# A hybrid decoder layer: the recurrence's output norm a block sooner, the matrix memory's norm turned into rows and spread by one-pass products

## The chip, the core and the metric

The kernel runs on one core of one Trainium2 chip. The metric is the time of one execution on the device in microseconds (us), median of several runs. A core has five engines that run beside each other, each through its own list of instructions in order: TensorE (PE, matrix products; PEld are its weight loads), VectorE (DVE), ScalarE (ACT), GpSimd (POOL) and SyncE (SP, which here only issues DMA transfers). They wait for each other by semaphores. Products land in PSUM, all else lives in SBUF.

## What is computed

One inference step of a decoder layer for 256 prompt tokens and 8 sample tokens, 264 columns together, model width 2048, all in float32. The reference, cut to the part that the change touches:

```python
z = rmsnorm(x, g_mix) @ w_in                       # one projection for all groups
h_rg, h_last = rglru(...)                          # gated linear recurrence, width 1024
y_rg = rmsnorm(h_rg * gelu(z[..., OFF_RGG:OFF_Q]), g_rg_out)
h_ml, C_new, n_new, m_new = mlstm(q, k, v, logi, logf, C0, n0, m0)   # 4 heads of 256
h_ml = rmsnorm(h_ml, g_ml_out.reshape(ML_HEADS, ML_DV))              # per token and head
y_ml = h_ml * jax.nn.sigmoid(z[..., OFF_O:OFF_I])
x = x + jnp.concatenate([y_rg, y_ml], axis=-1) @ w_out
```

Behind it come cross-attention to 256 memory tokens, a SwiGLU and a final norm. Two norms matter here: the one over the recurrence's 1024 channels, a number per token, and the one over the matrix memory's 256 channels, a number per token and head.

## The kernel before

Activations lie transposed, channels on the 128 partitions and the 264 tokens along the row. The weights stream through in steps: a list `steps` holds one entry for each block of 128 output channels, and the loop over it (L1430) loads a block two or three steps ahead, splits the block of the next step into a high and a low part that PE takes in one pass (`split_half`, L193: ACT makes the high part, DVE subtracts to get the low one, in two halves of 8 chunks each), runs the step's products, and then pumps side work. A block is 16 chunks of three products, `mm3`: high by high, high by low, low by high. So a step is 48 products of 128 by 264.

Steps 25 to 32 are the recurrence's gate blocks, 33 to 40 the matrix memory's output gates (`evac_o`, j = 0 to 7), and step 41 begins `w_out`, whose right side is the normed recurrence (chunks 0 to 7, `yrg`) and the gated matrix memory (chunks 8 to 15, `yml`).

Work that belongs to no block runs as generators beside the loop (`side`, `pump`). A yielded `STEP` ends a generator's turn; a number lets it go on if the engines' priced clocks have room. Products that such work needs are put between the chunks of a block through `later(f, after=n)` and `drip` (L282, L287): a function waits until n more chunks were recorded, is then recorded right there, and the next product of the block is ordered behind it. What is recorded is put into each engine's order by a list scheduler with its own estimates, except on SP, where it stays as written. The engines then keep that order.

The generators that matter:

- `rg_out` (L588): the recurrence's norm. `rstd_wide` (L384) splits the sum of squares `acc_rg` into halves, sums over the partitions by two products with a matrix of ones (the products stand in the program wherever the generator is pumped), and takes the inverse root by 9 DVE steps on 128x264. Then each of the 8 blocks is scaled and split into `yrg`.
- `ml_norm` (L873): the matrix memory's norm. Squares are summed per head in `a`; `sums(h)` brings the sums over the partitions, tokens on partitions, into 12 columns; the last `sums` forms f, a 128x12 vector (4 heads by 3 token windows), by a chain of short DVE operations. Behind it `spread` (L359) brings f back along the rows for each head: products of a broadcast column with the identity, 128x128, 128x128 and 128x8, in float32, each issued as two instructions. The 8 blocks of `hT` are scaled from PSUM.
- the loop keeps finished products in `pend` and runs their evacuation at the start of the next step, except where i is in a short list (L1440).

PSUM has four banks for blocks (`mm`) and four for side work (`ax`). Weight halves have four buffers (`W`), their raw loads five.

Of the kernel before, what the change touches and what calls it, by code (L numbers as in the profile page):

```python
# [10 lines left out]
F32 = mybir.dt.float32  # L11
F32R = mybir.dt.float32r
I32 = mybir.dt.int32
AF = mybir.ActivationFunctionType
# [3 lines left out]
P = 128  # L18
D = 2048
KC = D // P  # L20
T = 256
NS = 8
N = T + NS
RGB = 8
H = 4
# [19 lines left out]
STEP = object()  # L45
# [45 lines left out]
def layer_kernel(ctx: ExitStack, tc, xT, memT, vec, wrg, w_in, w_out, w_q, w_k, w_v, w_o,  # L91
# [3 lines left out]
    act, dve, pe = Engine(nc.scalar, price_act), Engine(nc.vector, price_dve), Engine(nc.tensor, price_pe)  # L95
# [10 lines left out]
    def nm(s):  # L106
        uid[0] += 1
        return f"{s}_{uid[0]}"
# [9 lines left out]
    def B(shape, dt=F32, skip=0):  # L118
        return view(sb.tile([P, SLOT], dt, tag="B", bufs=NB, name=nm("B")), shape, skip)
# [51 lines left out]
    steps = []  # L171
    LD, LS = 3, 1
    GATES = 8

    raws, splits = {}, {}

# [58 lines left out]
    st = {}  # L235
# [46 lines left out]
    def later(*fs, after=0):  # L282
        k = [after, list(fs)]
        drips.append(k)
        return k
# [13 lines left out]
    def bank(tag="mm"):  # L299
        return psm.tile([P, 512], F32, tag=tag, bufs=4, name=nm(tag))  # L300
# [4 lines left out]
    ident = const.tile([P, P], F32, name="ident")  # L305
# [3 lines left out]
    ones_r = const.tile([P, P], F32R, name="ones_r")  # L309
    dve.tensor_copy(ones_r, ones)  # L310
    ident_r = const.tile([4, H], F32R, name="ident_r")
# [47 lines left out]
    def spread(ps, c, n=N):  # L359

        for j in range(2 if n == T else 3):
            lo, hi = (j * P, j * P + P) if j < 2 else (T, N)
            i = pe.matmul(ps[:, lo:hi], c[j].to_broadcast([P, P]), ident[:, P - (hi - lo):], start=True, stop=True)
        return i
# [19 lines left out]
    def rstd_wide(acc, y, n):  # L384

        w = acc.shape[-1]
        hl, vt = B([P, 2, w], F32R), B([P, 3, w])
        act.activation(hl[:, 0], acc, AF.Copy)
        dve.tensor_sub(hl[:, 1], acc, hl[:, 0].bitcast(F32))
        yield STEP  # L390
        ps = bank("ax")
        for k in range(2):
            pe.matmul(ps[:, :w], ones_r, hl[:, k], start=k == 0, stop=k == 1)
        v, i, t = vt[:, 0], vt[:, 1].bitcast(I32), vt[:, 2]
        dve.tensor_scalar(v, ps[:, :w], 1.0 / n, EPS, op0=OP.mult, op1=OP.add)
        dve.tensor_single_scalar(i, v.bitcast(I32), 1, op=OP.logical_shift_right)
        dve.tensor_scalar(y.bitcast(I32), i, -1.0, 1597463007.0, op0=OP.mult, op1=OP.add)
        for _ in range(3):
            dve.tensor_mul(t, y, y)
            dve.scalar_tensor_tensor(t, t, -0.5, v, op0=OP.mult, op1=OP.mult)  # L400
            dve.scalar_tensor_tensor(y, t, 1.5, y, op0=OP.add, op1=OP.mult)
        yield 0.1

    def sumsq(acc, x, first):
        if first:
# [168 lines left out]
    acc_rg = const.tile([P, N], F32, name="acc_rg")  # L574
# [11 lines left out]
        return f  # L586

    def rg_out():  # L588
        yield STEP
        rr = ltmp()  # L590
        yield from rstd_wide(acc_rg, rr, RGB * P)
        st["yrg"] = HL(RGB)
        for n in range(RGB):
            h = rg["h"](n)
            dve.tensor_mul(h, h, rr)
            split(*st["yrg"](n), h, V("g_rg", n))
            yield 0.75


    ml = {}  # L600
# [272 lines left out]
    def ml_norm():  # L873

        while not (ml["pg"].done and ml["sg"].done) or st["i"] < 33:
            yield STEP
        hh = hT["t"]
        a = B([P, H, N])
        for h in range(H):
            for vb in range(2):  # L880
                act.activation(hh(2 * h + vb)[:, T:N], nums[:, 2 * h + vb, :], AF.Copy)
            sumsq(a[:, h, :], hh(2 * h), True)
            sumsq(a[:, h, :], hh(2 * h + 1), False)
            yield 0.35
        yield STEP
        ps = bank("ax")
        r, v, f = ctile(12), ctile(12), ctile(12)

        def sums(h):
            i = token_sums(ps, a[:, h, :], 3 * h)  # L890
            if h == 0:
                dve.tensor_max(r.rearrange("p (h j) -> p j h", j=3), den.rearrange("p (h j) -> p j h", j=3),
                               emc.rearrange("p (j h) -> p j h", h=H))
                dve.reciprocal(r, r)
                dve.tensor_mul(v, r, r)
            if h == H - 1:
                dve.scalar_tensor_tensor(v, ps[:, 0:12], 1.0 / 256, v, op0=OP.mult, op1=OP.mult)
                dve.tensor_scalar(v, v, EPS, None, op0=OP.add)
                rsqrt(v, f)
                dve.tensor_mul(f, f, r)  # L900
            return i

        for h in range(H):
            k = later(lambda h=h: sums(h), after=3 if h else 1)
        while k[1]:
            yield STEP
        for h in range(H):
            ps = bank("ax")
            spread(ps, [f[:, 3 * h + j: 3 * h + j + 1] for j in range(3)])
            for vb in range(2):  # L910
                dve.tensor_mul(hh(2 * h + vb), hh(2 * h + vb), ps[:, :N])
            yield 0.7
            ml["nn"] = h + 1

    def evac_o(j):
        def f(ps):
# [512 lines left out]
    pend = []  # L1429
    for i, (src, cols, pef, evf, need) in enumerate(steps):  # L1430
        load_piece(i + LD - 1)
        if i == 5:
            st["rg"] = side(rg_gen(), 0)
        if i == 6:
            finish(lambda: fn.done)
        for q in need:
            if q in st:
                finish(lambda: st[q].done)
        st["i"] = i
        if i not in (4, 5, 34, 35):  # L1440
            with tc.high_priority(300):
                for e, x in pend:
                    e(x)
            pend = []
        now = pe.clock
        dve.clock, act.clock = max(dve.clock, now), max(act.clock, now)
        parts = 2 if i == 0 else 1
        split_half(i + LS, 0, parts)
        if i + LS < len(steps) and steps[i + LS][1] > 1024:
            split_half(i + LS, 1, parts)  # L1450
        ps = pef(i)
        if 1 <= i < 4:
            with tc.issue_after(st["split"].ins):
                for q in ((0, 1), (2,), (3,))[i - 1]:
                    square(q)
        if i == 3:
            fn = side(first_norm(), -1)
        if i == 6:
            with tc.issue_after(st["split"].ins), tc.issue_after(st["low"].ins):
                rg_coef()  # L1460
        if evf is not None:
            pend.append((evf, ps))
        load_piece(i + LD)
        pump(pe.clock + SLACK)
        if i == 24:
            ml["ng"] = side(ml_norm(), -1)
        if i == len(steps) - 12:
            state_load()
        if i == 40:
            st["memg"] = side(mem_gen(), 7)  # L1470
# [4 lines left out]
    for lo, hi in ((0, 1), (1, 2), (2, 4), (4, 6), (6, 8), (8, 10), (10, 12), (12, 16)):  # L1475
        if lo == 12:
            state_store(3, 4)
        for c in range(lo, hi):
            e, r = (pool_e, rstd) if c in POOLC else (dve, fin["ps"][:, :N])
# [108 lines left out]
```

## Time and profile before

| | |
|---|---|
| three runs | 1541.16, 1540.39, 1539.16 us; median 1540.39 |
| the profiled execution's own time | 1540.57 us |
| its span (first to last instruction) | 1538.7 us |
| granted TensorE clock, mean | 0.997 |
| DMA | 329.17 MB, 214 GB/s on average |

In a row of a timeline stand start and duration in us, the engine, the program's line, the operation, what it writes and reads (tile names without numbers), the count, and in brackets the idle time before it with what ended it. In the chain of waits, the work that ended last is followed back from the end; its rows are start, duration, engine, tile and count. L63 is the line of a helper that records all instructions, so tile names and shapes tell them apart: `mm` is a block's PSUM bank, `ax` one of side work, `W` a split weight half, `raw` its load, `c` a tile of up to 16 columns, `t` and `lt` row tiles, `B` the large buffers. Durations of neighbouring rows of one engine overlap a little: the next starts before the former is written out.

### The profile page before, as it was taken

Reading aid. Unit: us, or ns where it says so; the run is one execution under the profiler, and the core shown is the slowest. Engines: PE = TensorE matmul, PEld = TensorE weight load, DVE = VectorE, ACT = ScalarE, POOL = GpSimd, SP = SyncE. Lnnn points to the kernel's source line nnn. Section 1 sums busy time; section 2 is a strip of 40 time slices with the busy share of each in tenths; the row PEclk is TensorE's granted clock in tenths of the full one; section 3 lists DMA queues with packets and bytes.
Section 4 is the critical chain, followed back from the end, with each engine's and each line's share of the span. In section 5 each row is a group of like instructions: output and inputs, shape, how many; then the busy total and the mean of one; then the engine's idle time right before and its main releaser. Section 6 shows DMA issues by size and latency. Waiting matters only on the chain.

```text
span 1538.7 us, 30018 instructions
## 1 busy us (share of the span) xinstructions
PE 1525.9 (99%) x12040; PEld 1492.1 (97%) x12040; DVE 1059.1 (69%) x2012; ACT 783.0 (51%) x1233; POOL 129.9 (8%) x195
## 2 busy tenths in 40 slices
PE   8999999999999999999999999999999999999997
PEld 8999999999998888899999999999999999999997
DVE  7976798878898989966665555455555554555554
ACT  6455775655555666654444443334444433344463
POOL 0001220000234334400000000000000000000000
PEclk9999999999999999999999999999999999999999
DMA  8655897556789798745555555555555555555473
GB/s 293 197 165 186 291 326 246 182 183 231 261 331 333 244 346 325 256 159 193 183 181 186 183 184 186 180 190 180 183 187 179 186 184 181 189 179 184 159 225 119
DMA packets 93659, 329.17 MB, mean 214 GB/s; under 512 B 10992, under 2 KB 11936, under 8 KB 93520
## 3 DMA queue, kind: packets, MB, share of 16 engines
q1 hardware_dynamic: 77760, 272.51, 53.0%
q0 software_dynamic: 15472, 54.22, 9.8%
q8 instruction: 94, 1.54, 0.4%
q10 hardware_dynamic: 288, 0.53, 0.1%
q14 instruction: 45, 0.37, 0.1%
HBM read 314.36 MB, written 12.86 MB: 213 GB/s over the span
## 4 chain that ended last, share of the span: by engine, by line
PE 97%; DVE 1%; DMA 1%; issue 0%; ACT 0%; POOL 0%; ACTq 0%; DVEq 0%
PE mm L63 92%; PE ax L63 5%; DVE B L63 1%; DMA B<-scr 0%; DMA xres<-xT 0%; DVE W L63 0%; DVE t L63 0%; ACT B L63 0%; POOL B L846 0%; ACTq L304 0%; DVE lt L63 0%; DVEq L1565 0%; ACT W L63 0%; ACT L63 0%; DVEq L63 0%
## 5 line engine op out<-in xcount | busy, mean ns | idle before, releaser
L63 PE MATMUL mm<-B,W 128*128 128x264 f32 (+2 forms) x11008 | 1363.3, 285 | 0.4 <-DVE W L63 0.4
L63 PEld LDWEIGHTS mm<-B,W 128*128 128x128 f32 x11008 | 1340.6, 188 | 12.3 <-DVE W L63 0.6
L63 ACT ACTIVATE W<-raw 128x1024 fp32r<-128x1024 f32 (+2 forms) x520 | 536.5, 1034 | 641.2 <-PE mm L63 438.5
L63 DVE TENSOR_TENSOR W<-raw,W 128x1024 fp32r<-128x1024 f32 (+2 forms) x520 | 620.4, 1195 | 348.8 <-ACT W L63 347.6
L63 PE MATMUL mm<-W,B 128*128 128x512 f32 x384 | 92.4, 395 | 0.0
L63 PEld LDWEIGHTS mm<-W,B 128*128 128x128 f32 x384 | 70.9, 188 | 16.2
L63 DVE TENSOR_TENSOR t<-mm,rstd 128x264 f32<-128x264 f32 x104 | 44.9, 433 | 43.8 <-PE mm L63 43.6
L1480 POOL TENSOR_TENSOR B<-B,rstd 128x264 f32<-128x264 f32 x4 | 2.8, 738 | 854.1 <-ACT rstd L63 854.1
L63 DVE TENSOR_TENSOR xres<-xres,mm 128x264 f32<-128x264 f32 (+1 forms) x81 | 34.3, 425 | 34.8 <-PE mm L63 34.7
L63 DVE SCALAR_TENSOR_TENSOR B<-B,dw 128x256 f32<-128x256 f32 x128 | 53.9, 477 | 1.8 <-ACT dw L63 1.7
L63 DVE SCALAR_TENSOR_TENSOR dw<-B,qsm,dw 128x256 f32<-128x256 f32 x96 | 50.7, 538 | 0.4
L1115 POOL TENSOR_TENSOR dr<-dw,dr 128x256 fp32r<-128x256 f32 x32 | 38.7, 1209 | 103.2 <-ACT dr L63 103.1
L63 PE MATMUL ax<-B,B 128*128 128x256 f32 (+2 forms) x272 | 44.7, 303 | 0.0
L63 PEld LDWEIGHTS ax<-B,B 128*128 128x128 f32 x272 | 38.5, 190 | 2.4
L63 ACT ACTIVATE B<-xres,vecs 128x264 fp32r<-128x264 f32 (+1 forms) x64 | 31.0, 502 | 2.2 <-DMA xres<-xT 2.0
L1104 POOL DMA_DIRECT2D B<-kcT x32 | 17.4, 543 | 134.8 <-DVE B L63 126.5
L63 ACT ACTIVATE t<-t 128x264 f32<-128x264 f32 (+1 forms) x61 | 24.7, 407 | 4.5 <-DVE t L63 4.5
L63 ACT ACTIVATE B<-t 128x264 fp32r<-128x264 f32 (+1 forms) x60 | 24.5, 408 | 4.5 <-DVE t L63 4.5
L63 ACT ACTIVATE t<-B,B 128x128 f32<-128x128 f32 x64 | 20.2, 388 | 12.0 <-DMA B<-scr 12.0
L63 ACT ACTIVATE t<-xres 128x264 f32<-128x264 f32 (+2 forms) x46 | 18.8, 410 | 14.6 <-DVE xres L63 14.6
L63 ACT ACTIVATE dw<-B,qsm 128x256 f32<-128x256 f32 x32 | 16.2, 508 | 18.3 <-DVE B L63 8.9
L63 DVE SCALAR_TENSOR_TENSOR B<-xres,vecs,B 128x264 fp32r<-128x264 f32 x48 | 22.4, 490 | 1.9 <-ACT B L63 1.9
(168 smaller groups left out, 663.6 us busy)
## 6 DMA issues: line engine op xcount, KB each, us to landing
raw<-w_gu SPq DMA_DIRECT2D x176, 512.0 KB, 3.6
raw<-w_d SPq DMA_DIRECT2D x80, 512.0 KB, 3.7
raw<-w_in SPq DMA_DIRECT2D x78, 512.0 KB, 5.0
raw<-w_out SPq DMA_DIRECT2D x32, 512.0 KB, 3.7
raw<-w_q SPq DMA_DIRECT2D x32, 512.0 KB, 5.4
B<-kcT POOLq DMA_DIRECT2D x32, 512.0 KB, 7.9
B<-vcT POOLq DMA_DIRECT2D x32, 512.0 KB, 8.3
raw<-w_k SPq DMA_DIRECT2D x32, 512.0 KB, 6.3
```

The source lines that it names most:

```text
L63: return f(*a, **k)
L1104: pool_e.dma_start(kc, kcT[h, b])
L1115: pool_e.tensor_sub(wr[:, 1], acc, wr[:, 0].bitcast(F32))
L1480: e.tensor_mul(st["y"](c), st["y"](c), r)
```

## The change

Five edits. In `rstd_wide` the generator yields its last product, so that it can be recorded as a drip. `rg_out` makes the halves at once, then records products and inverse root 13 chunks later by a drip; its eight scalings wait for the steps in `RGAT` and are ordered behind the latest weight split. `ml_norm` puts all four sums two chunks apart; 19 further chunks on, `turn` brings f from columns to rows, a 4x264 tile, by three products with the identity, ACT and DVE split it into halves, and from six chunks later `scale(h)` spreads each head by two one-pass products of 4 rows, and scales its two blocks. The loop holds the evacuation of steps 33, 34 and 35 until the products of step 36 are recorded.

```diff
@@ -171,6 +171,7 @@
     steps = []
     LD, LS = 3, 1
     GATES = 8
+    RGAT = (34, 34, 34, 37, 38, 38, 39, 39)
 
     raws, splits = {}, {}
 
@@ -390,7 +391,7 @@
         yield STEP
         ps = bank("ax")
         for k in range(2):
-            pe.matmul(ps[:, :w], ones_r, hl[:, k], start=k == 0, stop=k == 1)
+            last = pe.matmul(ps[:, :w], ones_r, hl[:, k], start=k == 0, stop=k == 1)
         v, i, t = vt[:, 0], vt[:, 1].bitcast(I32), vt[:, 2]
         dve.tensor_scalar(v, ps[:, :w], 1.0 / n, EPS, op0=OP.mult, op1=OP.add)
         dve.tensor_single_scalar(i, v.bitcast(I32), 1, op=OP.logical_shift_right)
@@ -399,7 +400,7 @@
             dve.tensor_mul(t, y, y)
             dve.scalar_tensor_tensor(t, t, -0.5, v, op0=OP.mult, op1=OP.mult)
             dve.scalar_tensor_tensor(y, t, 1.5, y, op0=OP.add, op1=OP.mult)
-        yield 0.1
+        yield last
 
     def sumsq(acc, x, first):
         if first:
@@ -586,13 +587,19 @@
         return f
 
     def rg_out():
-        yield STEP
         rr = ltmp()
-        yield from rstd_wide(acc_rg, rr, RGB * P)
+        wide = rstd_wide(acc_rg, rr, RGB * P)
+        next(wide)
+        k = later(lambda: next(wide), after=13)
+        while k[1]:
+            yield STEP
         st["yrg"] = HL(RGB)
         for n in range(RGB):
+            while st["i"] < RGAT[n]:
+                yield STEP
             h = rg["h"](n)
-            dve.tensor_mul(h, h, rr)
+            with tc.issue_after(st["low"].ins):
+                dve.tensor_mul(h, h, rr)
             split(*st["yrg"](n), h, V("g_rg", n))
             yield 0.75
 
@@ -900,17 +907,37 @@
                 dve.tensor_mul(f, f, r)
             return i
 
+        fp = bank("ax")
+        hl = B([P, 2, N], F32R)[0:4]
+
+        def turn():
+            fj = f.rearrange("p (h j) -> p j h", j=3)
+            for j, w0 in enumerate((0, P, T)):
+                w = min(P, N - w0)
+                i = pe.matmul(fp[0:4, w0: w0 + w], fj[:, j, :], ident[:, P - w:], start=True, stop=True)
+            act.activation(hl[:, 0], fp[0:4, :N], AF.Copy)
+            dve.tensor_sub(hl[:, 1], fp[0:4, :N], hl[:, 0].bitcast(F32))
+            return i
+
+        def scale(h):
+            ps = bank("ax")
+            sel = ident_r[:, h: h + 1].to_broadcast([4, P])
+            for k in range(2):
+                i = pe.matmul(ps[:, :N], sel, hl[:, k], start=k == 0, stop=k == 1)
+            with tc.issue_after(st["low"].ins):
+                for vb in range(2):
+                    dve.tensor_mul(hh(2 * h + vb), hh(2 * h + vb), ps[:, :N])
+            ml["nn"] = h + 1
+            return i
+
         for h in range(H):
-            k = later(lambda h=h: sums(h), after=3 if h else 1)
+            later(lambda h=h: sums(h), after=1)
+        for h in range(H):
+            if h == 0:
+                later(turn, after=19)
+            k = later(lambda h=h: scale(h), after=1 if h else 6)
         while k[1]:
             yield STEP
-        for h in range(H):
-            ps = bank("ax")
-            spread(ps, [f[:, 3 * h + j: 3 * h + j + 1] for j in range(3)])
-            for vb in range(2):
-                dve.tensor_mul(hh(2 * h + vb), hh(2 * h + vb), ps[:, :N])
-            yield 0.7
-            ml["nn"] = h + 1
 
     def evac_o(j):
         def f(ps):
@@ -1437,7 +1464,7 @@
             if q in st:
                 finish(lambda: st[q].done)
         st["i"] = i
-        if i not in (4, 5, 34, 35):
+        if i not in (4, 5, 34, 35, 36):
             with tc.high_priority(300):
                 for e, x in pend:
                     e(x)
@@ -1449,6 +1476,11 @@
         if i + LS < len(steps) and steps[i + LS][1] > 1024:
             split_half(i + LS, 1, parts)
         ps = pef(i)
+        if i == 36:
+            with tc.high_priority(300):
+                for e, x in pend:
+                    e(x)
+            pend = []
         if 1 <= i < 4:
             with tc.issue_after(st["split"].ins):
                 for q in ((0, 1), (2,), (3,))[i - 1]:
```

What the scheduler makes of it, engine by engine. Numbers behind names tell buffers apart. In PE's list `mm_359` is the block of step 34, `ax` a side bank, `ones_r` the matrix of ones. Before, PE has the recurrence's two products in step 37 (block `mm_393`), behind its first half:

```order
L63 MATMUL mm_393_3327<-B_17_165,W_383_3245 128x264
L63 MATMUL mm_393_3327<-B_16_164,W_383_3245 128x264
L63 MATMUL ax_377_3210<-B_364_3092,ones_r_78 128x264 [waits DVE_49,PE_49]
L63 MATMUL ax_377_3210<-B_364_3092,ones_r_78 128x264
L63 MATMUL mm_393_3327<-B_18_174,W_384_3248 128x264 [waits Activation_49]
```

Now they stand in step 34, six products before its end:

```order
L63 MATMUL mm_359_3039<-B_21_185,W_345_2947 128x264
L63 MATMUL mm_359_3039<-B_20_184,W_345_2947 128x264
L63 MATMUL ax_360_3082<-B_355_3029,ones_r_78 128x264 [waits PE_49,Activation_49]
L63 MATMUL ax_360_3082<-B_355_3029,ones_r_78 128x264 [waits DVE_49]
L63 MATMUL mm_359_3039<-B_20_184,W_345_2947 128x264
L63 MATMUL mm_359_3039<-B_21_185,W_345_2947 128x264
```

The pair moved three steps up; the second product has a wait of its own for DVE.

DVE's list, the end of the chain that makes f (`c_362`, now `c_366`). Before, one weight split (`W_384`) stands in the chain's second half:

```order
L63 SCALAR_TENSOR_TENSOR c_362_3090<-c_370_3165,c_362_3090 128x12 [waits DVE_49]
L63 TENSOR_TENSOR c_370_3165<-c_362_3090 128x12 [waits DVE_49]
L63 TENSOR_TENSOR W_384_3248<-raw_358_3085,W_384_3248 128x8x128 [waits DMAHW0_49,Activation_49]
L63 SCALAR_TENSOR_TENSOR c_370_3165<-c_370_3165,c_361_3089 128x12 [waits DVE_49]
L63 SCALAR_TENSOR_TENSOR c_362_3090<-c_370_3165,c_362_3090 128x12 [waits DVE_49]
```

Now the recurrence's inverse root and three of its scalings (`B_184`, `B_370`) and two splits (`W_379`, `W_393`) stand in it, and the 4x264 subtraction follows:

```order
L63 SCALAR_TENSOR_TENSOR B_370_3115<-B_184_1700,vecs_68,B_369_3114 128x264 [waits Activation_49]
L63 SCALAR_TENSOR_TENSOR c_375_3169<-c_375_3169,c_365_3109 128x12 [waits DVE_49]
L63 TENSOR_TENSOR W_379_3217<-raw_362_3105,W_379_3217 128x8x128 [waits DMAHW0_49,Activation_49]
L63 SCALAR_TENSOR_TENSOR c_366_3110<-c_375_3169,c_366_3110 128x12 [waits DVE_49]
L63 SCALAR_TENSOR_TENSOR B_370_3115<-B_184_1700,vecs_68,B_369_3114 128x264 [waits Activation_49] x2
L63 TENSOR_TENSOR c_375_3169<-c_366_3110 128x12 [waits DVE_49]
L63 SCALAR_TENSOR_TENSOR c_375_3169<-c_375_3169,c_365_3109 128x12 [waits DVE_49]
L63 TENSOR_TENSOR W_393_3324<-raw_376_3204,W_393_3324 128x8x128 [waits DMAHW1_49,Activation_49]
L63 SCALAR_TENSOR_TENSOR c_366_3110<-c_375_3169,c_366_3110 128x12 [waits DVE_49]
```

So the recurrence's work moved from behind f to ahead of it and between its steps; the order of DVE, ACT and PE up to the pair in step 34 is the same in both kernels.

PE's list at the start of `w_out`. Before, products of step 42 (`mm_432`) stand among those of step 41 (`mm_421`):

```order
L63 MATMUL mm_421_3606<-B_389_3306,W_413_3535 128x264 [waits DVE_49]
L63 MATMUL mm_421_3606<-B_388_3305,W_413_3535 128x264
L63 MATMUL mm_421_3606<-B_396_3384,W_413_3535 128x264 [waits Activation_49]
L63 MATMUL mm_432_3679<-B_388_3305,W_419_3600 128x264 [waits DVE_49]
L63 MATMUL mm_432_3679<-B_388_3305,W_419_3600 128x264
L63 MATMUL mm_432_3679<-B_389_3306,W_419_3600 128x264
```

Now step 41 (`mm_423`) runs on at that place:

```order
L63 MATMUL mm_423_3609<-B_370_3115,W_415_3538 128x264
L63 MATMUL mm_423_3609<-B_369_3114,W_415_3538 128x264
L63 MATMUL mm_423_3609<-B_406_3454,W_415_3538 128x264
L63 MATMUL mm_423_3609<-B_407_3455,W_415_3538 128x264
L63 MATMUL mm_423_3609<-B_406_3454,W_415_3538 128x264 x2
```

The mixing of the two blocks moved to the last two gate chunks of step 41; past it PE's list is the old one again. SP's and POOL's lists are the same.

## The prediction

> **What bounds the kernel now.** I read the page first, then who PE waits for, then the chain of waits and the engines' timelines around the edited steps.
>
> ```profile
> span 1538.7 us, 30018 instructions
> PE 1525.9 (99%) x12040; PEld 1492.1 (97%) x12040; DVE 1059.1 (69%) x2012; ACT 783.0 (51%) x1233; POOL 129.9 (8%) x195
> PE mm L63 <- DVE W L63: 0.4, 1, 0.4
> ```
>
> TensorE (PE) is busy 99% of the span. Away from start and end it idles at two places, 0.6 us near 163 us and 0.4 us near 279 us. So the change can win only what it takes off PE's own stream plus that 0.4 us, and every new PE wait adds in full. The chain around the edited steps is all PE:
>
> ```profile
> 201.62 35.49 PE mm L63 x294
> 237.11 0.56 PE ax L63 x6
> 237.67 1.56 PE mm L63 x12
> ...
> 243.49 0.56 PE ax L63 x6
> 244.05 7.20 PE mm L63 x59
> 251.25 2.58 PE ax L63 x24
> 253.82 2.38 PE mm L63 x19
> 256.20 0.24 PE ax L63 x2
> 256.44 14.38 PE mm L63 x120
> ```
>
> A block product takes 35.49/294 = 0.1207 us, a block of 48 takes 5.79. The first x6 group is the first of four norm sums and stands 6 products into step 35, so step 35 starts at 236.39 and step 34 at 230.60. Behind the last sum 6 products remain, so step 36 starts at 244.77 and step 37 at 250.56. Step 37 holds the x24 group (matrix-memory spread, 2.58) and the x2 group (recurrence norm, 0.24); step 38 starts at 256.44 + 24 x 0.1207 = 259.34.
>
> **The recurrence norm, moved from step 37 into step 34.** Its two products now stand behind 42 of step 34's 48: PE is there at 237.11 - 12 x 0.1207 = 235.66. They read the high and low half of the recurrence's sum of squares.
>
> ```profile
> 234.89 0.41 ACT L63 ACTIVATE B<-acc_rg 128x264 fp32r<-128x264 f32 x1
> 235.69 1.22 DVE L63 TENSOR_TENSOR W<-raw,W 128x1024 fp32r<-128x1024 f32 x1
> 236.82 0.43 DVE L63 TENSOR_TENSOR B<-acc_rg,B 128x264 fp32r<-128x264 f32 x1
> 238.01 1.23 DVE L63 TENSOR_TENSOR W<-raw,W 128x1024 fp32r<-128x1024 f32 x1 [0.75 <-ACT W L63]
> 278.79 21.44 PE L63 MATMUL mm<-B,W 128*128 128x264 f32 x176 [0.42 <-DVE W L63]
> ```
>
> The high half is there at 235.30. The low half is not: VectorE (DVE) makes it behind a weight split, until 237.25, and up to this row DVE, ACT and PE have the same order in both kernels. Before, the product came 19 us later and this was hidden. Now the second product waits for it. PE gets there at 235.78 and goes on at 237.30 (0.05 after the operation, as behind the split of 277.51 that ends at 278.74): **stall 1 is 1.5 us**, between 1.4 and 1.7. All of PE's stream is queued behind it.
>
> **The matrix-memory norm.** The four sums now stand two chunks apart, the same four interruptions. The vector f behind them is a chain of 14 short DVE operations; before it was ready at 248.4, 2.8 us ahead of its use:
>
> ```profile
> 244.29 0.59 DVE L63 TENSOR_SCALAR c<-c 128x12 f32<-128x12 f32 x3
> 248.23 0.17 DVE L63 TENSOR_TENSOR c<-c,c 128x12 f32<-128x12 f32 x1
> 258.53 0.49 DVE L63 SCALAR_TENSOR_TENSOR B<-t,vecs,B 128x264 fp32r<-128x264 f32 x1
> 258.94 0.30 DVE L63 TENSOR_SCALAR B<-B 128x264 int32<-128x264 int32 x1
> 259.14 1.30 DVE L63 SCALAR_TENSOR_TENSOR B<-t,vecs,B 128x264 fp32r<-128x264 f32 x3
> 260.36 0.43 DVE L63 TENSOR_TENSOR t<-mm,rstd 128x264 f32<-128x264 f32 x1
> 260.70 0.29 DVE L63 TENSOR_SCALAR lt<-B 128x264 int32<-128x264 int32 x1
> 260.90 1.23 DVE L63 TENSOR_TENSOR W<-raw,W 128x1024 fp32r<-128x1024 f32 x1
> 262.04 0.43 DVE L63 TENSOR_TENSOR B<-lt 128x264 f32<-128x264 f32 x1
> 265.45 0.42 DVE L63 TENSOR_TENSOR B<-lt 128x264 f32<-128x264 f32 x1
> 265.91 0.43 DVE L63 SCALAR_TENSOR_TENSOR B<-B 128x264 f32<-128x264 f32 x1
> ```
>
> In the new order DVE runs, from 238.01 to f: 5 weight splits at 1.14 (260.90 to 262.04), 5.70; 7 wide steps whose successor needs them at 0.46 (265.45 to 265.91), 3.22; 8 other wide ones at 0.345 (260.36 to 260.70), 2.76; 3 with a gain vector at 0.41 (258.53 to 258.94), 1.23; 2 integer ones, 0.5; 5 short ones at 0.2 (0.59 for three dependent), 1.0, and nine between other work, 0.8 in all (0.09 is the part of the 0.17 that isn't overlapped). The sum is 15.2, **f ready at 253.25**. DVE never pauses there: by the same count its splits' ACT halves, the sums and step 35's end come 0.1 to 1.5 us before they are needed.
>
> PE reaches the turn, 36 products into step 36, at 237.42 + 6 x 0.1207 + (244.77 - 236.39) + 36 x 0.1207 = 250.87. It waits to 253.3, and as f is the weights here a load of 0.19 follows, which can't run ahead (its row stands below): **stall 2 is 2.6 us**. If short operations cost nothing and nothing waits in the chain, it is 1.2; if every short one takes 0.2 and each wait adds some, 3.4. I take the count.
>
> **PE's own work.** Out goes the x24 group: steps 37 and 38 are 8.78 apart, 48 products 5.79, the x2 group 0.24, so it and its interruption cost 2.75. In come a turn of 6 instructions and 8 one-pass products; the latter's nearest rows, 4 rows of weights on 256 columns:
>
> ```profile
> 147.10 0.29 PEld L63 LDWEIGHTS ax<-B,ident_r 4*128 4x128 f32 x2
> 147.10 0.50 PE L63 MATMUL ax<-B,ident_r 4*128 4x256 f32 x2
> 147.53 0.92 PE L63 MATMUL ax<-B,B 128*128 128x256 f32 x4
> L63 PEld LDWEIGHTS ax<-ident,c 128*128 128x128 f32 x48 | 5.7, 190 | 0.3 <-DVE c L63 0.3
> ```
>
> A pair holds PE 0.43 instead of 0.24, but its two loads follow each other within 0.11, so the extra is paid on entering and leaving. Eight in a row: 8 x 0.12 + 0.28 = 1.25; between 0.96 and 1.75 (8 x 0.215). The turn: 6 at 2.58/24 = 0.1075 and 0.15 for the interruption, 0.8; between 0.2 and 0.95. Net -0.7, between -1.6 and 0.
>
> The Trainium skill, "TensorE: Matmul & The Clock Gate", section "LDWEIGHTS (loading the stationary operand)", says a weight load takes time by its columns and not by its rows. The spread's 0.1075 per instruction agrees with its 107 ns for 128 columns; the turn's weights have 4 columns, and by the rule it would cost about 0.3 (an estimate by that page) in place of 0.8, the sum 0.5 less.
>
> **The wait at 279.** Before, a product of step 42 stood inside step 41 and waited for its weights' low half behind the recurrence's scalings. In the new order step 41 runs through first and the scalings lie over steps 36 to 39: -0.4. What is late next: each later split is due at least 2 us before PE by the same count (step 39's first done at 264, used at 268).
>
> **At nothing.** One more small copy and subtraction (0.41 and 0.43, as the rows of 234.89 and 236.82) lie under the 12 products between turn and scaling, with 0.3 us to spare; without that cover 0.8. The eight scalings only move. Gates held till step 36: their block's bank is needed again three steps later. POOL's last two memory-token loads wait for later buffers, but are read only after step 43. The moved parts issue no transfer; SP's weight loads wait for splits that come a few us later and have over 10 us left.
>
> **Sum.** 1.5 + 2.6 - 0.7 - 0.4 = +3.0, against the profiled execution's own 1540.57 us (span 1538.7) 1543.6, against the median of 1540.39 1543.4; I say **1543.5**. About 0.2% (3.08 us) is what a measurement of this kernel can tell from no change, and the forecast lies on that line. By the ends of the terms it is +0.7 to +5.1.
>
> **Rivals.**
> Not slower: f is in time. If DVE's queue to f is 2 us or more shorter than counted, stall 2 shrinks to its weight load or a little more and the sum is +0.2 to +1, 1541.2. It decides where DVE reaches f by 250.9. For it: before, f took 4.3 us with one split in its way. Against: five splits and the whole recurrence norm now lie ahead, and DVE's queue is in order.
>
> Clearly slower: the clock. At the start of the span PE ran slow:
>
> ```profile
> 6.40:12.00 5.60, 3.93 (x18) 3.73 (x19) 4.62 (x11) 4.95 (x12) 0.00 (x0) 0.70 1.01 361
> 8.46 3.99 PE ax L63 x19
> ```
>
> The granted clock was 0.70 there and a product took 0.21. If stall 2 brings that back for as many products, 19 x 0.09 = 1.7 more, 1545.2; it decides from a stall of a length that no row here shows (0.6 us at 163 did nothing). The page named above, "Part 1: The HAM clock gate", has the clock fall after an idle window of about 3.4 us; by that rule 2.6 us isn't enough, which is why this stays a small rival.
>
> The change does what it says: no stall at either place, only -0.7 - 0.4, 1539.3. Against it stands the low half's row at 236.82.
>
> **How the numbers follow.** Forecast 0.70 (1541.9 to 1545, half of it beyond the line), f in time 0.13, clock 0.13, neither stall 0.04. Slower by over 0.2%: 0.36 + 0.13 = 0.49; faster 0.03, only if a gain I don't see joins the last case; the rest 0.48 is within. The range 1541.1 to 1545.7 takes in the terms' ends but for the corners, the upper rival and most of the lower.
>
> **What would show it.** In PE's waits, after: one of 1.5 us for DVE on B near 236 and one of 2 to 3 for DVE on c near 251; none near 279; x24 gone, an x6 and an x8 group around 254 to 257. Wrong if PE's waits stay under 1 us, if step 38 starts before 261, or if the granted clock dips.

## The result and the profile after

| | before | changed |
|---|---|---|
| median in the same series | 1540.74 us (8 runs, 1539.16 to 1541.28) | 1544.47 us (8 runs, 1541.12 to 1547.05) |
| ratio, 95% interval | | 1.0025 (1.0015 to 1.0034), that is +3.9 us (+2.3 to +5.2) |
| the profiled execution | 1540.57 us, span 1538.7 | 1543.46 us, span 1541.7 |

All medians and ratios here are of runs in the faster of the two states in which this program runs; of all experiments only the pair later had others, two of its eleven runs (1663.11 and 2529.84 us).

The page of the changed kernel, its span and engines:

```profile
span 1541.7 us, 29995 instructions
PE 1526.2 (99%) x12030; PEld 1491.8 (97%) x12030; DVE 1059.3 (69%) x2013; ACT 784.1 (51%) x1234; POOL 129.3 (8%) x195
```

PE is busy almost as long as before (1526.2 against 1525.9 us); most of the 3.0 us of span is idle time. PE's waits in the changed kernel (total in us, times, longest):

```profile
PE ax L63 <- ACT B L63: 2.9, 1, 2.9
PE ax L63 <- DVE c L63: 2.2, 1, 2.2
PE ax L63 <- DVE B L63: 1.2, 2, 0.7
```

The wait for DVE on `W` near 279 is gone, the one for `c`, which holds f, is new. PE's timeline at the two edited places:

```profile
236.69 0.29 PE L63 MATMUL ax<-B,ones_r 128*128 128x264 f32 x1
237.47 0.39 PE L63 MATMUL ax<-B,ones_r 128*128 128x264 f32 x1 [0.49 <-DVE B L63]
...
253.56 0.63 PE L63 MATMUL ax<-ident,c 128*4 128x128 f32 x6 [2.20 <-DVE c L63]
254.12 1.70 PE L63 MATMUL mm<-B,W 128*128 128x264 f32 x12
255.76 1.22 PE L63 MATMUL ax<-B,ident_r 4*128 4x264 f32 x8
256.91 43.29 PE L63 MATMUL mm<-B,W 128*128 128x264 f32 x359
```

And DVE's, the low half, the split behind it, and the last operation of f:

```profile
236.98 0.43 DVE L63 TENSOR_TENSOR B<-acc_rg,B 128x264 fp32r<-128x264 f32 x1
238.17 1.23 DVE L63 TENSOR_TENSOR W<-raw,W 128x1024 fp32r<-128x1024 f32 x1 [0.76 <-ACT W L63]
253.24 0.17 DVE L63 TENSOR_TENSOR c<-c,c 128x12 f32<-128x12 f32 x1
```

Both stalls are where the prediction put them: 0.49 us at the pair, 2.20 at the turn. f came at 253.41 (forecast 253.25). The turn, the spreading and what they interrupt take 256.91 - 253.56 less 12 products of 0.1207, 1.9 us, where the x24 group took 2.75: 0.8 less.

Yet these don't add up to a plain 3.0. PE reached the pair 1.2 us later than the same place stood in before, although all engines have one order up to there. So the executions differ ahead of the change, and the spans alone don't tell what it costs. A second profile of each kernel, and those of the experiments, tell more. I take the start of step 34 from each profile, and the time from there to the end of the span:

| kernel | span | step 34 starts | from there to the end | against before | low half, after that start |
|---|---|---|---|---|---|
| before | 1538.7 | 230.60 | 1308.1 | | 6.65 |
| before, again | 1540.2 | 232.12 | 1308.1 | 0.0 | 5.26 |
| changed | 1541.7 | 231.79 | 1309.9 | +1.8 | 5.62 |
| changed, again | 1542.6 | 233.58 | 1309.0 | +0.9 | 3.05 |
| changed, third | 1541.0 | 231.07 | 1309.9 | +1.8 | 5.60 |
| changed, fourth | 1541.5 | 230.94 | 1310.6 | +2.5 | 4.58 |
| scalings later | 1538.4 | 231.46 | 1306.9 | -1.2 | 4.60 |
| both later, the turn too | 1537.9 | 230.96 | 1306.9 | -1.2 | 4.86 |
| pair and scalings later | 1537.1 | 228.84 | 1308.3 | +0.2 | 5.14 |
| recurrence only | 1539.2 | 231.11 | 1308.1 | 0.0 | 5.65 |
| twelve products | 1540.7 | 231.85 | 1308.9 | +0.8 | 3.91 |
| pair later | 1542.7 | 230.86 | 1311.8 | +3.7 | 5.26 |
| turn early | 1543.7 | 230.62 | 1313.1 | +5.0 | 3.98 |
| turn early, PE busy | 1541.9 | 230.29 | 1311.6 | +3.5 | 4.36 |

The start is that of the recurrence's pair in PE's timeline, plus 0.17 (the chain of waits of the kernel with twelve products has at 236.92 what the timeline has at 236.75), less the products of 0.1207 ahead of it: 42, or 51 or 54 where an experiment moved the pair. For before it is the prediction's 230.60, and for its second profile 1.52 more, as its first x6 group shows below. The last column is the end of DVE's row `B<-acc_rg,B`, less that start.

### The profile page after: what moved, and what is told of

It reads as the page before. It is cut to its first block, busy times and chain, and to the rows that moved or that the text cites. A ratio compares the mean times of both kernels' runs of the same rounds, so it can differ in the third digit from the quotient of the medians.

```text
span 1541.7 us, 29995 instructions
## 1 busy us (share of the span) xinstructions
PE 1526.2 (99%) x12030; PEld 1491.8 (97%) x12030; DVE 1059.3 (69%) x2013; ACT 784.1 (51%) x1234; POOL 129.3 (8%) x195
## 4 chain that ended last, share of the span: by engine, by line
PE 94%; DVE 2%; DMA 2%; issue 1%; ACT 1%; ACTq 0%; POOL 0%; DVEq 0%
PE mm L63 90%; PE ax L63 5%; DMA B<-scr 1%; DVE B L63 1%; DVE W L63 1%; DVE t L63 0%; DMA xres<-xT 0%; ACT W L63 0%; ACT t L63 0%; ACT B L63 0%; DVE c L63 0%; DVE lt L63 0%; DVE acc_rg L63 0%; POOL B L853 0%; ACTq L305 0%
```

## The experiments

**The scalings later.** The first three scalings of the recurrence out of f's way, the products where they were.

```diff
-    RGAT = (34, 34, 34, 37, 38, 38, 39, 39)
+    RGAT = (37, 37, 37, 37, 38, 38, 39, 39)
```

> The changed kernel, with its first three scalings of the recurrence held until step 37 (RGAT begins 37, 37, 37 in place of 34, 34, 34). On DVE three scalings with 128x264 products, three with the gain vector and one weight split then stand behind f and no longer ahead of it; the products keep their order. By the count of the prediction f is ready at 250.0 in place of 253.3, and PE is at the turn at 250.9 or later. Theory: PE starts the turn when DVE has f, so the wait for DVE on c falls from 2.2 us to under 0.3; the wait for the low half near 237 stays as it was (0.5 to 1.5, by how late PE gets there). Time 1541.2 (1540.7 to 1542.0), that is 2.2 to 3.2 less than the changed kernel. Rival, that the 3.4 us lost at the turn come from something else (the products of four weight columns, the banks, the gates held): the time stays at 1543 or above and the wait for c, or an idle stretch at that place, stays over 1.5 us.

Measured: 1539.35 us, ratio 0.9992 (0.9983 to 1.0001). PE's timeline, and DVE's for the end of f:

```profile
236.36 0.41 PE L63 MATMUL ax<-B,ones_r 128*128 128x264 f32 x2
250.19 0.64 PE L63 MATMUL ax<-ident,c 128*4 128x128 f32 x6
```

```profile
248.97 0.17 DVE L63 TENSOR_TENSOR c<-c,c 128x12 f32<-128x12 f32 x1
```

f is there at 249.1, a microsecond ahead of PE, and both waits are gone. What is left of the change is -1.2 from step 34 on: the prediction's -0.4 and the measured -0.8. So the turn, the four columns, the banks and the held gates cost nothing that shows; the wait for f does. Against the expectation, which had 1540.7 to 1542.0, the first wait went too, since in this execution the low half came 1 us earlier against PE than in the changed kernel's first profile. With the scalings one weight split, the last ahead of f, moved behind f as well; what it does shows further down.

**The recurrence's half alone.** The new `rg_out` and `RGAT`, with `ml_norm` and the hold of the gates as before.

```diff
-        if i not in (4, 5, 34, 35, 36):
+        if i not in (4, 5, 34, 35):
...
+            spread(ps, [f[:, 3 * h + j: 3 * h + j + 1] for j in range(3)])
```

> The recurrence's half of the change alone: its two products in step 34, its root and its scalings at the steps of RGAT. The matrix memory's norm is that of before (float32 spread, now at the end of step 37), and so is the hold of the gates. DVE's list to f is as long as in the changed kernel, but PE needs f only at the end of step 37, at about 258, with f ready at 255.4 by the count. Theory, the wait for c comes from needing f 36 products into step 36, not from the recurrence's work as such: no wait for c over 0.3 us, a wait for B near 237 of 0 to 1.5 us (more where PE arrives early against DVE), none near 279. From the start of step 34 to the end that is -0.4 to +1.1 us against before, time 1540.3 to 1541.8, ratio 0.9997 to 1.0007. Rival, that the recurrence's move costs what the changed kernel loses, wherever f is needed: 1543 or more.

Measured: 1539.52 us, ratio 0.9992 (0.9982 to 1.0002). PE's timeline, then DVE's:

```profile
236.01 0.29 PE L63 MATMUL ax<-B,ones_r 128*128 128x264 f32 x1
236.82 0.39 PE L63 MATMUL ax<-B,ones_r 128*128 128x264 f32 x1 [0.53 <-DVE B L63]
...
257.75 2.74 PE L63 MATMUL ax<-ident,c 128*128 128x128 f32 x24
```

```profile
255.03 0.17 DVE L63 TENSOR_TENSOR c<-c,c 128x12 f32<-128x12 f32 x1
```

f comes even later, at 255.2, and PE doesn't wait for it: it needs it at 257.75. From step 34 on the kernel is even with before: 0.53 lost at the pair, 0.4 won at 279. The time is 0.8 us below the range that I expected; from step 34 on it is within it. The recurrence's move by itself is nearly free. It costs where the matrix memory's f stands behind it in DVE's queue and is needed in step 36.

**The pair later.** Do the two stalls add up?

```diff
-        k = later(lambda: next(wide), after=13)
+        k = later(lambda: next(wide), after=16)
-                later(turn, after=19)
+                later(turn, after=16)
```

> The changed kernel, with the recurrence's two products three chunks later (after=13 becomes 16), the sums and the turn shifted with them so that the turn stands 30 products into step 36 in place of 36. PE then gets to the pair when the low half is ready or nearly so. Rival, the two stalls add up, as the prediction's sum has them: the first stall goes, the second stays at about 2.2 to 2.6 us, and the time falls by 0.5 to 1.5 us against the changed kernel. Theory, both stalls end at a time that DVE's list sets, so that an earlier stall only shortens the later one: the wait for B near 237 falls under 0.4, the wait for c grows to 3 to 4.5 us, and the time is that of the changed kernel or up to 1.0 us more (six more products lie behind f, 0.7 us): 1543.8 to 1545.5. If the wait for c is over 3.4 us the granted clock may also show a dip behind it.

Measured: 1544.46 us (median of nine runs), ratio 1.0027 (1.0017 to 1.0038), within what the theory expected and the same as the changed kernel's 1544.47. PE's timeline, a window of 6 us around it (length, busy time and instructions of PE, PEld, DVE, ACT, POOL, then the granted clock and the DMAs), and DVE's end of f:

```profile
236.85 0.40 PE L63 MATMUL ax<-B,ones_r 128*128 128x264 f32 x2
252.39 1.05 PE L63 MATMUL ax<-ident,c 128*4 128x128 f32 x6 [3.46 <-DVE c L63]
253.37 3.44 PE L63 MATMUL mm<-B,W 128*128 128x264 f32 x18
```

```profile
249.00:255.00 6.00, 2.61 (x13) 2.26 (x14) 3.46 (x12) 0.75 (x2) 0.00 (x0) 0.77 0.53 175
```

```profile
252.08 0.17 DVE L63 TENSOR_TENSOR c<-c,c 128x12 f32<-128x12 f32 x1
```

The wait at the pair is gone and nothing is won: f came 15.4 us after DVE began the split behind the low half (236.87 to 252.25), as in the changed kernel's first profile (238.17 to 253.41, 15.2). PE, with 15 products fewer between pair and turn, waits that much longer. So in these two executions f is timed by DVE's queue, and moving the turn forward only moves the wait. The second finding wasn't in the sum: behind 3.46 us of idle time the granted clock was 0.77, the turn took 1.05 us in place of 0.63, and 18 products took 3.4 us in place of 2.2.

**Twelve products ahead of the turn.** PE works in the time in which it would wait.

```diff
         def turn():
             fj = f.rearrange("p (h j) -> p j h", j=3)
+            for _ in range(12):
+                pe.matmul(fp[:, :N], ones_r, st["xn"](0)[0], start=True, stop=True)
```

> The changed kernel, with twelve extra products of 128x264 by the matrix of ones recorded directly ahead of the turn; they are written to the bank that the turn overwrites. PE's own work grows by 12 x 0.1207 = 1.45 us, and all engines but PE have the order of the changed kernel. Theory, f sets the time: the wait for c falls from 2.2 to about 0.75 us and the time stays within 0.3 us of the changed kernel. Rival, PE's own work counts and the wait is moved along: the wait for c stays at 2.2 us and the time is 1.45 us more. A third: if the long idle stretch of PE costs clock afterwards, the shorter wait makes this kernel faster than the changed one, by up to 1.5 us.

Measured: 1542.48 us, ratio 1.0011 (1.0002 to 1.0020). PE's timeline, and a row of its chain of waits for the pair:

```profile
236.75 0.41 PE L63 MATMUL ax<-B,ones_r 128*128 128x264 f32 x2
250.49 1.61 PE L63 MATMUL ax<-B,ones_r 128*128 128x264 f32 x12
252.58 0.64 PE L63 MATMUL ax<-ident,c 128*4 128x128 f32 x6 [0.47 <-DVE c L63]
```

```profile
236.92 0.24 PE ax L63 x2
```

The wait shrank to 0.47, and from step 34 on the kernel is no slower than the changed one (+0.8 against +0.9 to +2.5): 1.45 us of added work are hidden. Its median lies 2.0 and 0.9 us below those of the changed kernel in two other series, on the side of the third expectation, but the intervals of the ratios overlap (1.0002 to 1.0020 here, 1.0015 to 1.0034 and 1.0007 to 1.0025 there).

**The pair and the scalings later.** Both waits were to go.

```diff
-    RGAT = (34, 34, 34, 37, 38, 38, 39, 39)
+    RGAT = (37, 37, 37, 37, 38, 38, 39, 39)
-        k = later(lambda: next(wide), after=13)
+        k = later(lambda: next(wide), after=17)
-                later(turn, after=19)
+                later(turn, after=17)
```

> The changed kernel, with the first three scalings held until step 37 and the recurrence's two products four chunks later (after=17), the turn kept at 36 products into step 36. By the count of the prediction the low half is there 0.2 us ahead of the pair and f is ready at about 250.4, ahead of PE at 250.9. Theory: neither wait is left (each under 0.3 us), PE's own work is 0.8 us less than before and the wait near 279 stays gone: 1539.5 (1538.8 to 1540.4), 0.4 to 1.6 us less than before the change and some 4 to 5 less than the changed kernel. Rival: a wait for a weight split or for a scaled block turns up behind step 37, since eleven wide operations now stand there in DVE's list, and the time is 1540.5 to 1542.

Measured: 1540.12 us, ratio 0.9996 (0.9987 to 1.0005). The time is within what I expected, but the wait for c, which was to be under 0.3 us, was 1.20. PE's timeline, then DVE's:

```profile
248.87 0.63 PE L63 MATMUL ax<-ident,c 128*4 128x128 f32 x6 [1.20 <-DVE c L63]
```

```profile
247.41 1.23 DVE L63 TENSOR_TENSOR W<-raw,W 128x1024 fp32r<-128x1024 f32 x1 [0.33 <-ACT W L63]
248.56 0.16 DVE L63 TENSOR_TENSOR c<-c,c 128x12 f32<-128x12 f32 x1
```

One weight split got between f's last two operations, and waited 0.33 us for its ACT half. With its 1.14 that is more than the 1.20 that PE lost. Why this ACT half comes no sooner, the changed kernel's further profiles show below.

**Both later, the turn too.** The same with the pair a chunk sooner and the turn a chunk later, an order in which that split stands behind f.

```diff
-        k = later(lambda: next(wide), after=17)
+        k = later(lambda: next(wide), after=16)
-                later(turn, after=17)
+                later(turn, after=19)
```

> The changed kernel, with the first three scalings held until step 37 (RGAT begins 37, 37, 37), the recurrence's two products three chunks later (after=16) and the turn at 39 products into step 36 (after=19, counted from sums that stand a chunk later). By the count f is ready at 250.05 and PE at the turn at 251.2; the low half is there at 237.25 at the latest and PE at the pair at 236.8. Theory: no wait over 0.4 us at either place, PE's own work 0.8 us less than before the change and the wait near 279 gone: 1539.5 (1538.8 to 1540.2), 1.2 us less than before, as e1_scalings_later or a little less. Rival: nine products between turn and spreading don't cover the copy and the subtraction (0.94 us in the changed kernel), and a weight split now stands between them: up to 0.7 us more.

Measured: 1539.23 us, ratio 0.9991 (0.9983 to 1.0000); beside it in one series the changed kernel had 1543.35. PE's timeline:

```profile
236.95 0.40 PE L63 MATMUL ax<-B,ones_r 128*128 128x264 f32 x2
250.05 0.64 PE L63 MATMUL ax<-ident,c 128*4 128x128 f32 x6
```

No wait is left at either place, and the -1.2 from step 34 on is the same as with the scalings later alone. These two are the best versions: 4 us faster than the changed kernel, against before less than such a comparison can tell.

**The changed kernel again, three times.**

> The changed kernel once more, beside the three that follow, to compare its time and its spread with theirs. Theory: DVE's place in time differs from execution to execution by up to 1.6 us (in the five profiled executions so far the low half near 236 was made 1.3 to 1.6 us sooner or later against PE, following when a transfer landed near 157 us), so the wait for c differs too, between 1 and 3.5 us; where it passes a length between 2.2 us (clock 1.00 in the changed kernel) and 3.46 us (clock 0.77 in the kernel with the pair later) a slower clock costs about 1.5 us more. Expected median 1543.5 to 1544.5, spread from 1541 to 1547, the times with the lower mean clock among the longest.

> The changed kernel, a third profiled execution, to see whether its two waits and the clock behind them differ from execution to execution. From step 34 to the end the two profiles so far lie 1.8 and 0.9 us above before, the medians 3.9 and 2.5. Theory, the wait for c is always 2.0 to 2.2 us at full clock and only the wait for B varies (0 to 1.5): +0.9 to +2.4 from step 34 on, granted clock 1.00 between 249 and 261. Rival, the clock drops behind a wait of 2 us in some executions: if so here, under 0.95 in one of those windows and 1.5 us more.

> The changed kernel, a fourth profiled execution, for the same question and with the same numbers as the third.

Measured: again 1543.35 us (12 runs, 1541.20 to 1547.11), ratio 1.0016 (1.0007 to 1.0025); third and fourth 1542.72 and 1543.26, a single run each. The mean clock of a run didn't tell the long ones: 0.996 at 1547.11 and 0.997 at 1541.20. (In the first series the longest run, 1547.05, had the lowest, 0.993.) PE's timeline of the second, the third and the fourth profile:

```profile
238.48 0.41 PE L63 MATMUL ax<-B,ones_r 128*128 128x264 f32 x2
254.40 0.63 PE L63 MATMUL ax<-ident,c 128*4 128x128 f32 x6 [2.02 <-DVE c L63]
```

```profile
236.73 0.39 PE L63 MATMUL ax<-B,ones_r 128*128 128x264 f32 x1 [0.47 <-DVE B L63]
252.82 0.63 PE L63 MATMUL ax<-ident,c 128*4 128x128 f32 x6 [2.20 <-DVE c L63]
```

```profile
235.84 0.41 PE L63 MATMUL ax<-B,ones_r 128*128 128x264 f32 x2
251.76 1.04 PE L63 MATMUL ax<-ident,c 128*4 128x128 f32 x6 [2.02 <-DVE c L63]
252.73 2.83 PE L63 MATMUL mm<-B,W 128*128 128x264 f32 x12
```

and the windows of the fourth, with those of the first for comparison:

```profile
249.00:255.00 6.00, 3.98 (x23) 3.43 (x22) 2.86 (x10) 0.83 (x2) 0.00 (x0) 0.73 0.53 175
```

```profile
249.00:255.00 6.00, 3.80 (x33) 3.49 (x32) 4.60 (x14) 2.45 (x5) 0.00 (x0) 1.00 0.56 182
```

The wait at the turn is 2.0 to 2.2 in all four, where I had expected 1 to 3.5; that at the pair is 0.5 in two and absent in two. It is odd that the former hardly differs: in the second profile the low half came 2.6 us earlier against PE than in the first (3.05 and 5.62 in the table), so if DVE's queue alone timed f, the wait would have been nearly gone. Three rows of the second profile show what else holds f back, the 60 products between the last norm sum and the turn in PE's timeline, then a row each of ACT's and DVE's:

```profile
244.95 7.43 PE L63 MATMUL mm<-B,W 128*128 128x264 f32 x60
```

```profile
251.03 1.06 ACT L63 ACTIVATE W<-raw 128x1024 fp32r<-128x1024 f32 x1 [0.69 <-ACT t L63]
```

```profile
252.12 1.23 DVE L63 TENSOR_TENSOR W<-raw,W 128x1024 fp32r<-128x1024 f32 x1 [0.45 <-ACT W L63]
```

These are the ACT and the DVE half of the last weight split ahead of f. DVE idled 0.45 us for ACT's, and ACT had idled 0.69 before it, though its operation before (`t`) was done when that idle time began. In all four profiles the ACT half starts 6.08 to 6.10 us after the first of the 60 products: behind 48 of them (5.79), that is when PE has passed 24 products of step 36, the first half of its weights. From there to the turn it is 3.37 us in the second and the fourth profile and 3.55 in the others, and PE has only 12 products, 1.45 us, to do. So about 2 us of waiting are left however early DVE is; DVE's queue adds the last 0.2, in the two executions with a wait at the pair. The cause is argued and not shown by a run of its own: weight halves have four buffers, so the first half of step 38 can only be split into the buffer that the first half of step 36 gives up. The experiments fit it: with this split behind f the wait was gone (the scalings later), with it between f's last two operations 1.20 were left (the pair and the scalings later).

In the fourth the clock fell, to 0.73 on average in the window, behind a wait of 2.02 us, with which the second profile ran on at full clock: the turn cost 0.4 and the 12 products 1.1 us more. So the clock rival does come to pass, in one of these four executions.

**The turn early, and the same with PE kept busy.**

```diff
-                later(turn, after=19)
+                later(turn, after=11)
```

> The changed kernel, with the turn eight chunks sooner (after=19 becomes 11: 12 products into step 36 in place of 36). PE is there at about 248.4 and f, by the count, at 252.1 to 252.3. Theory without a clock cost: the wait for c is 3.7 to 4.2 us, 24 more products (2.9 us) lie behind it, f is 1.0 us sooner, and the spread products stand in four pairs apart (0.2 us each): some 2.5 us more than the changed kernel, 1546 to 1547. With the clock cost seen in the kernel with the pair later (18 products in 3.38 us in place of 2.17, and the turn in 1.05 in place of 0.63): 1.5 us more again, 1547.5 to 1549, and the granted clock near 255 under 0.9.

> The kernel with the turn early, with 24 extra products of 128x264 recorded directly ahead of the turn and written to the bank that the turn overwrites: PE's own work grows by 24 x 0.1207 = 2.9 us, and DVE's list up to f is the same. Theory, f sets the time and a long idle stretch costs clock: the wait for c falls from about 3.9 to about 1.0 us, the granted clock near 255 is 1.00, and the kernel is about 1.5 us FASTER than the one without the extra products, 1546 to 1547. Rival, no clock cost: the same time as without them (within 0.5 us). Rival, the extra products count: 2.9 us slower.

The second adds 24 products where the kernel above has twelve. Measured: 1545.78 us, ratio 1.0035 (1.0022 to 1.0047), and 1545.30, 1.0028 (1.0017 to 1.0040). PE's timeline and window of the first, then of the second:

```profile
249.88 0.63 PE L63 MATMUL ax<-ident,c 128*4 128x128 f32 x6 [3.33 <-DVE c L63]
250.45 4.33 PE L63 MATMUL mm<-B,W 128*128 128x264 f32 x21
```

```profile
249.00:255.00 6.00, 5.12 (x29) 4.87 (x29) 1.43 (x6) 1.44 (x2) 0.00 (x0) 0.72 0.22 76
```

```profile
246.06 3.07 PE L63 MATMUL ax<-B,ones_r 128*128 128x264 f32 x24
249.69 0.64 PE L63 MATMUL ax<-ident,c 128*4 128x128 f32 x6 [0.56 <-DVE c L63]
250.26 2.78 PE L63 MATMUL mm<-B,W 128*128 128x264 f32 x21
```

```profile
249.00:255.00 6.00, 5.44 (x41) 4.62 (x40) 2.81 (x9) 1.44 (x2) 0.00 (x0) 1.00 0.23 75
```

With 24 products more PE got through the same stretch sooner: behind the turn 21 products took 2.78 us in place of 4.33. From step 34 on it is +3.5 against +5.0, so the clock cost 1.5 us. The medians have the sign, but differ by 0.5 us in place of 1.5, and their intervals overlap. The wait was 3.33 and not 3.7 to 4.2, and the time 2 to 3 us below what I expected with the clock cost: part of it is that the changed kernel's median, to which I had added, holds more than its profile.

**Before, again.**

> The kernel before the change, unchanged: what the comparison shows for no difference, and a second profile of it. The profiled executions so far, all of one order up to step 34, start that step anywhere from 228.7 to 233.7 us, so expected is a ratio within 0.999 to 1.001, a start of step 34 other than the 230.6 of the first profile, and from there to the end the same time within 0.3 us as in the first profile, with the wait near 279 there again (0.2 to 0.6 us).

Measured: 1540.70 us, ratio 1.0002 (0.9993 to 1.0011). The first norm sum and the wait near 279, in PE's timeline of the second and of the first profile:

```profile
238.47 0.72 PE L63 MATMUL ax<-ones,B 128*128 128x1 f32 x6
280.27 9.93 PE L63 MATMUL mm<-B,W 128*128 128x264 f32 x80 [0.42 <-DVE W L63]
```

```profile
236.95 0.72 PE L63 MATMUL ax<-ones,B 128*128 128x1 f32 x6
```

The sum came 1.52 us later and the span ended 1.5 us later. So between these two executions the whole difference arises ahead of step 34, and what follows takes the same time.

## Why the prediction was right, and where not

The time lay in the range and the forecast 1 us from the median; both stalls, what went, and their places are as predicted, though the first stall was there in only two of four profiles. The sizes are not all.

**Stall 1, "1.5 us, between 1.4 and 1.7"**: 0.49, 0, 0.47 and 0 in the four profiles. This term was mis-sized. The step read the low half's lateness from one execution, and that was the latest of all: 6.65 us after the start of step 34, where the other 13 profiles show 3.05 to 5.65. PE needs it at 42 x 0.1207 + 0.12 = 5.19.

**Stall 2, "2.6 us"**: 2.0 to 2.2 of idle time. The sums of the table leave 0.1 to 0.3 more; rows of one engine overlap by up to 0.17, so an idle stretch is shown that much shorter than the delay is. The count of DVE's queue, 15.2 us, came out as 15.2, 15.2 and 15.3 in three of the profiles, and as 16.5 in the second. The step "DVE never pauses there" failed in that one: DVE paused 0.47 us for PE's last sum and 0.45 for the ACT half of the last weight split. The prediction set such waits aside. But that split began in no profile before PE was 24 products into step 36, and this alone gives about 2 us; that it lies within 0.2 us of what DVE's queue gives is luck.

**PE's own work, "net -0.7"**: -0.8. The turn, the spreading and their interruptions took 1.9 where I had 0.8 and 1.25. By the rule of the Trainium skill, "TensorE: Matmul & The Clock Gate", section "LDWEIGHTS (loading the stationary operand)", that a load takes time by its columns, the turn would have cost 0.3 (the prediction's estimate). The trace agrees only in direction about the loads, whose rows are 0.085 us long with 4 columns and 0.189 with 128 (0.107 by the rule), and not about the turn: its six instructions took 0.63/6 = 0.105 us each, those of the spread 0.1075.

**The wait at 279, -0.4, and the edits at nothing**: so it is. The two kernels without waits end 1.2 us sooner from step 34 on, which is 0.8 + 0.4.

**The rivals.** f in time is the better version: 1539.2 to 1539.4 where f came before PE, below the rival's 1541.2 since no stall 1 was left. The clock, given 0.13, was kept small for the wrong reason: it was set aside because 2.6 us isn't an idle window of about 3.4 us, the length that the same page of the Trainium skill, section "Part 1: The HAM clock gate", names. The trace doesn't agree: a wait of 2.02 us brought 0.73.

So the sum of +3.0 came out near the measured +3.9 and +2.5 partly by luck. Stall 1 was 1.0 to 1.5 us too large in it. From step 34 on the four profiles show only +0.9 to +2.5, of which 1.5 is clock where it fell. That the medians lie higher still, by 1 to 2 us, isn't settled. A drop in more than one of four executions could explain part of it; no profile was taken of the others. The ends of the terms add up to +0.6 and +4.7 and not to +0.7 and +5.1, which changes nothing here.

## What to carry to other kernels

A vector that a chain of short operations makes on an in-order engine is as late as everything queued between them, and as late as what that work itself waits for, a buffer that PE has yet to free included: count both before you bring its use forward, and hold back what isn't due yet. Read a stall's length from several executions, at a place common to both kernels; from one, it is a sample. Here a wait of PE of 1.5 us or more could cost a slower clock on top, and idle time filled with useless products was cheaper than idle time.

## What had not been expected of the hardware

The granted clock fell behind idle stretches of PE of 2.02 us (0.73 in the window of 6 us, in one of four), 3.33 (0.72) and 3.46 (0.77), and not behind 2.02, 2.20 and 2.20 in the others. It can fall behind a shorter one: the second profile of the changed kernel has a drop ahead of step 34, behind 1.51 us. Its row in PE's timeline and a window of 3 us behind it:

```profile
171.84 1.65 PE L63 MATMUL ax<-B,B 128*128 128x256 f32 x4 [1.51 <-ACT B L63]
```

```profile
172.00:175.00 3.00, 3.00 (x12) 2.82 (x13) 2.11 (x7) 2.97 (x8) 0.00 (x0) 0.50 1.03 412
```

Where nothing slowed them, in the fourth profile, the same four products took 0.92 us behind 1.05 us of idle time. Between 100 and 300 us, stretches of 1.28 us and less brought no drop in any of the profiles. In all four of these drops the clock stood at 0.50, for 3.4 us by windows of half a microsecond to one; each of the three behind the turn cost about 1.5 us. What decides whether a stretch of 1.5 to 2.2 us brings one isn't shown.

The 14 executions, whose order is the same up to there, reach step 34 between 228.8 and 233.6 us, and DVE's place against PE's varies there by 3.6 us. They differ ahead of it in PE's idle time: 1.6 to 3.1 us in a wait near 8 us, and 0 to 2.2 us between 160 and 175 us. What sets these wasn't tried.
